# A two-layer hybrid decoder trunk: hand-over times per layer, rotary tables made first, row halves alternating in the Gram and score products

## The chip, the cores and the metric

The kernel runs on one core of one Trainium2 chip. The metric is the device time of one execution in microseconds (us); smaller is better. The core has a matrix engine (TensorE, PE in the profile; its weight loads are PEld), a vector engine (VectorE, DVE), an activation engine (ScalarE, ACT), a general engine (GpSimd, POOL) and a queue that issues most transfers (SyncE, SP). Each engine takes its instructions in the order in which they stand in its queue.

## What is computed

Two decoder layers over 512 tokens of width 1024, float32. Each layer runs three mixers side by side on one projection, adds their sum, and then a SwiGLU:

```python
for l in range(DEPTH):                       # DEPTH = 2
    hn = rms_norm(h, attn_norm[l])
    proj = hn @ w_in[l]                      # 1024 -> 2592
    y_a, v_first = rwkv7_mixer(...)          # 4 heads x 64, a delta-rule state per token
    y_b = retention_mixer(...)               # 4 heads x 64, chunks of 128, rotary q and k
    y_c = mla_mixer(...)                     # 8 heads, latent q / kv, one rotary key for all
    h = h + concat(y_a, y_b, y_c) @ w_out[l]
    gu = rms_norm(h, ffn_norm[l]) @ w_gate_up[l]
    h = h + (silu(gu[..., :D_FF]) * gu[..., D_FF:]) @ w_down[l]   # D_FF = 2816
return rms_norm(h, final_norm)
```

The RWKV-7 mixer's recurrence, for each head and token t, is

```python
sa = einsum('bhvk,bhk->bhv', state, -kkt)
state = state * wt + sa (x) (kkt * at) + vt (x) kt
y = einsum('bhvk,bhk->bhv', state, rt)
```

with kk the key direction brought to unit length. Rotary embedding multiplies by cos and sin of position times frequency.

## The kernel before

**Activations and GEMMs.** Activations lie transposed, channels on the 128 partitions and the 512 tokens along the row. Each weight block of 1024x128 (512 KB) is loaded by SP into a tile wr, rounded by ACT into wh (line 375) and its remainder formed into wl by DVE or POOL (line 376). An activation is kept as two such halves as well, and a product is three passes (high by high, high by low, low by high), 24 matmuls of 128x512 for a block: tiles pd<-u,wh and pd<-u,wl, all of them at line 231, the helper mm. Transposes are at line 238, the helper tr.

**What sets the order on PE.** `dense` is the main stream: it walks through the GEMMs of both layers. Beside it run tasks, Python generators: `tables` (cos and sin), `rwkv`, `chain`, `group_norm`, `retnet`, eight `head` tasks, `attend`, `key_rope`, `latent_norm`, `norm`. A `Driver` holds them with a priority and goes on with the first whose wait is over. A task yields either a condition or a number, the amount of modelled PE time that must pass before it continues; the numbers stand in the table T. So T sets where between the GEMM matmuls a task's products are put. PE keeps that order exactly; what the other engines do is ordered by a scheduler that follows from the same program.

**The RWKV task.** After the low-rank products (line 295 makes the halves of their input) it squares the scaled keys, sums them by head with a product by `blk` (the key norm: line 547 reads it, the rsqrt helper's lines 326 to 329 follow, line 548 multiplies), and forms decayed operands AR and BK per chunk of 64 tokens (DVE 605 to 607, POOL 608, 609). Then come the Gram matrices. Two heads share 128 partitions, 64 rows each (a row half, `par`); for each of 2 halves, 2 blocks and 2 chunk quartets, four matmuls of 64x128 go into one PSUM bank (tile pm), and DVE writes two masked copies of it (lines 632, 633, tiles GL and GR). Four PSUM banks serve all tiles named pm in turn. Behind the Gram matrices stand the bonus products (line 641 reads them) and the transposes of BK. A substitution of 31 steps of two DVE operations (lines 679, 680) inverts triangles; then the chain runs over eight chunks, with a copy R on ACT (729), a negated copy uv on ACT (733) and the state Sb on DVE (746, 748) between its products.

**RetNet and the rest.** The q and k blocks are multiplied by the norm's factor rB (DVE, line 978), four transfers on SP swap the rotary halves, POOL multiplies by cos and sin (981, 982) and DVE adds (983). `retnet` builds three chunk states: transpose, a decayed copy kt (DVE 794), product, masked copy Rs; then the score products of 64 rows, four matmuls to a bank, one bank for each head. Line 817 of its norm forms the low half that the next product reads. `key_rope` rotates the shared MLA key with six small DVE operations (1010 to 1015, tile kro) and transposes it. `tables` reads the positions and makes three sets of angles, the RetNet ones, a token-major set for the shared key and the MLA ones; the operations at 435 to 450 reduce each angle, ACT takes the sine.

Of the kernel before, what the change touches and what calls it, by code (L numbers as in the profile page):

```python
# [44 lines left out]
def shape_constants():  # L45
    """Constants that depend on shapes and hyper-parameters alone."""
# [39 lines left out]
# rows of the parameter matrix (one row = 128 consecutive values of a parameter)  # L86
# [15 lines left out]
class Driver:  # L102
    """Orders the PE stream: the first task whose wait (in PE time, or a condition) is over goes on."""
# [25 lines left out]
def lay_out(inp):  # L129
    """The inputs as the kernel reads them: reshapes, transposes and repeated columns only."""  # L130
# [47 lines left out]
def tile_trunk(ctx: ExitStack, tc: tile.TileContext, a: dict, out: bass.AP, dbg=None):  # L178
# [50 lines left out]
    def mm(o, lhsT, rhs, start=True, stop=True, cost=None):  # L229
        """A matmul that keeps its place in the PE stream."""  # L230
# [76 lines left out]
    def norm_feed(t, g, acc, tag="acc"):  # L307
        """Square of tile t into acc and the g-scaled tile as an exact hi/lo pair."""
# [14 lines left out]
    def rsqrt(x, y=None):  # L323
        """1 / sqrt(x) of a whole tile, with one Newton step."""
# [7 lines left out]
    def inv_rms(accs, n, tag):  # L332
        """rsqrt(mean + eps) per token, the same in all partitions, from tiles of squares."""
# [7 lines left out]
    def norm(acc, st):  # L341
        yield T["norm1"]
# [9 lines left out]
    # the weights, in order of use, as exact hi/lo pairs two blocks ahead of their products  # L352
# [31 lines left out]
    def gemm(ps, w, x, ks, first=True, last=True, wsl=None):  # L384
        """ps += w^T x in three exact passes; ks = [(index in w, index in x)]."""
# [13 lines left out]
    def first_two(x):  # L399
        """Two products whose last contraction tile comes late."""  # L400
# [16 lines left out]
    def tables():  # L417
        yield T["tables1"]
# [9 lines left out]
        def angles(inv, tok=False):  # L428
# [10 lines left out]
            yield T["angles1"]  # L439
            rest = TWO_PI  # L440
            for bits in (7, 9, 9, None):
# [7 lines left out]
                yield T["angles2"]  # L449
            dve.tensor_scalar(ang, ang, 3.1415925, -3.1415925, ALU.min, ALU.max)  # L450
            yield T["angles3"]
# [5 lines left out]
            yield T["angles4"]  # L457
# [7 lines left out]
        yield T["angles5"]  # L465
        yield from angles(None, True)
        ready["kr"] = True
        yield T["angles6"]
# [8 lines left out]
    def rwkv(l, st):  # L477
        rkv = st["rkv"]
        yield lambda: "xs1" in st
        yield T["rwkv1"]  # L480
# [16 lines left out]
        yield T["rwkv2"]  # L497
# [15 lines left out]
        yield T["rwkv3"]  # L513
        aa = ur([P, 2, S])
        gg = sm((P, 2, S), tag="gg", bufs=1)
        for rows, dst, bias in ((slice(32, 64), aa, "rw_a0"), (slice(64, 128), gg, None)):
            for b in range(2):
# [9 lines left out]
                yield T["rwkv4"]  # L527
        st["gg"] = gg

        # unit key direction  # L530
        yield lambda: "k" in rkv
        k_ = rkv["k"]
        yield T["rwkv5"]
# [8 lines left out]
        yield T["rwkv6"]  # L542
        for b in range(2):
# [5 lines left out]
            yield T["rwkv7"]  # L549
        # k' = k (1 + (a - 1) k_a),  b = kk a  # L550
# [10 lines left out]
        else:  # L561
            vf = ur([P, 2, S])
            sp.dma_start(vf, vf_d)
            yield T["rwkv8"]
# [5 lines left out]
            yield T["rwkv9"]  # L570
            for b in range(2):
# [7 lines left out]
                yield T["rwkv10"]  # L579

        # decays, centred on the middle of each chunk
# [6 lines left out]
        for b in range(2):  # L588
            Ein, Eex, Einv = r2(), r2(), r2()
            for i in range(2):  # L590
# [12 lines left out]
                yield T["rwkv11"]  # L603
# [12 lines left out]
        yield T["rwkv12"]  # L616
# [631 lines left out]
```

## Time and profile before

| | |
|---|---|
| median of 3 runs | 1428.18 us (1426.40 to 1428.36) |
| profiled execution, first to last instruction (its own time; no other is on the page) | 1423.1 us |
| instructions | 17218 |
| TensorE busy, matmuls | 1366.6 us, 96% |
| TensorE's weight loads | 1074.5 us, 76% |
| VectorE / ScalarE / GpSimd busy | 799.1 / 566.5 / 267.2 us |
| mean granted TensorE clock | 0.970 |
| moved by transfers | 130.85 MB, mean 92 GB/s |

The page states busy time per engine, and the granted clock as a share of full speed. A row of a timeline gives start, length, engine, line, operation, output<-inputs, shapes, count, and in brackets how long the engine was idle before it and whose result ended that. Matmuls are pipelined, so records overlap, and each float32 matmul of the small products shows as two records.

### The profile page before, as it was taken

The page shows a single profiled execution, that of the slowest core. Times are in us where ns is not written, and L with a number is a line of the kernel's source. Part 1 is how long each engine was busy: PE and PEld are TensorE (multiplying, and loading weights), DVE is VectorE, ACT ScalarE, POOL GpSimd, SP SyncE. Part 2 cuts the span into 40 slices and gives each one's busy share as a digit, 9 for nine tenths or more (in the row PEclk, how much of TensorE's full clock was granted, in tenths as well). Part 3 has the DMA queues.
Part 4 walks back from the last instruction along what each step waited for, and adds up shares of the span by engine and source line. Part 5 has one row for each costly group of instructions (what it writes and reads, how often), then busy time and mean ns, then how long its engine had stood idle before and what let it go on. Part 6 is the DMA issues. An engine that isn't in the chain of part 4 may idle for free.

```text
span 1423.1 us, 17218 instructions
## 1 busy us (share of the span) xinstructions
PE 1366.6 (96%) x6622; PEld 1074.5 (76%) x6622; DVE 799.1 (56%) x1167; ACT 566.5 (40%) x943; POOL 267.2 (19%) x233
## 2 busy tenths in 40 slices
PE   7989899899999999999999989999999999999996
PEld 5768666568788888888887776765788888888884
DVE  6665855775644345444556767657475434543443
ACT  7633353663432223222457134448263322322233
POOL 2142024222211011001213502332031200100111
PEclk9869999999999999999999899999999999999998
DMA  6324231202332232322342332312123333333321
GB/s 224 90 81 112 76 92 53 91 36 77 104 102 95 98 98 95 103 89 93 118 138 77 107 87 56 100 43 75 59 89 104 89 104 93 100 98 95 100 77 60
DMA packets 61738, 130.85 MB, mean 92 GB/s; under 512 B 24948, under 2 KB 27668, under 8 KB 61656
## 3 DMA queue, kind: packets, MB, share of 16 engines
q1 hardware_dynamic: 60280, 128.14, 29.1%
q8 instruction: 52, 0.85, 0.3%
q10 hardware_dynamic: 1232, 1.09, 0.2%
q0 software_dynamic: 144, 0.52, 0.1%
q14 instruction: 30, 0.25, 0.1%
HBM read 117.40 MB, written 9.18 MB: 89 GB/s over the span
## 4 chain that ended last, share of the span: by engine, by line
PE 83%; DVE 8%; ACT 4%; issue 3%; POOL 1%; DMA 0%; SPq 0%; DVEq 0%; ACTq 0%; POOLq 0%
PE pd L231 70%; PE pm L231 12%; PE pm L238 1%; DVE r L680 1%; ACT wh L375 1%; DVE u L320 1%; DVE r L679 1%; DMA wr<-in_wts_dram 0%; DVE wl L376 0%; ACT u L860 0%; DVE nmx L858 0%; DVE u L286 0%; DVE r L295 0%; DVE r L328 0%; DVE r L329 0%
## 5 line engine op out<-in xcount | busy, mean ns | idle before, releaser
L231 PE MATMUL pd<-u,wh 128*128 128x512 f32 x3048 | 963.6, 397 | 9.9 <-ACT wh L375 6.3
L231 PEld LDWEIGHTS pd<-u,wh 128*128 128x128 f32 x3048 | 571.2, 190 | 139.8 <-issue 8.3
L231 PE MATMUL pd<-u,wl 128*128 128x512 f32 x1524 | 598.8, 393 | 0.0
L375 ACT CAST wh<-wr 128x1024 fp32r<-128x1024 f32 (+3 forms) x206 | 208.6, 1015 | 547.0 <-PE pd L231 349.2
L231 PEld LDWEIGHTS pd<-u,wl 128*128 128x128 f32 x1524 | 289.3, 190 | 61.3 <-DVE wl L376 0.2
L376 DVE TENSOR_TENSOR wl<-wr,wh 128x1024 fp32r<-128x1024 f32 (+3 forms) x198 | 277.6, 1404 | 82.9 <-ACT wh L375 82.1
L1184 POOL TENSOR_TENSOR r<-r,r 128x512 f32<-128x512 f32 x44 | 62.3, 1416 | 584.3 <-ACT wh L375 337.5
L1183 DVE TENSOR_TENSOR r<-pd,rB 128x512 f32<-128x512 f32 x44 | 30.4, 691 | 133.7 <-PE pd L231 133.7
L1190 DVE TENSOR_TENSOR u<-u,pd 128x512 f32<-128x512 f32 x48 | 33.0, 687 | 125.8 <-PE pd L231 125.8
L231 PE MATMUL pm<-u,u 32*32 32x32 f32 (+7 forms) x856 | 97.3, 279 | 5.8 <-DVE u L607 4.3
L231 PEld LDWEIGHTS pm<-u,u 32*32 32x32 f32 (+4 forms) x856 | 70.1, 155 | 41.5 <-issue 25.2
L315 POOL TENSOR_TENSOR acc<-acc,r 128x512 f32<-128x512 f32 x37 | 56.8, 1534 | 221.5 <-ACT r L314 221.0
L1181 DVE TENSOR_TENSOR r<-pd,rB 128x512 f32<-128x512 f32 x44 | 30.4, 691 | 68.4 <-PE pd L231 68.3
L285 ACT CAST u<-r 128x512 fp32r<-128x512 f32 x52 | 32.2, 622 | 63.0 <-POOL r L1184 62.8
L231 PE MATMUL pd<-u,u 96*128 96x512 f32 (+3 forms) x128 | 47.7, 471 | 1.9 <-ACT u L860 1.3
L286 DVE TENSOR_TENSOR u<-r,u 128x512 fp32r<-128x512 f32 x52 | 36.4, 701 | 16.5 <-ACT u L285 16.3
L376 POOL TENSOR_TENSOR wl<-wr,wh 128x1024 fp32r<-128x1024 f32 (+1 forms) x8 | 19.7, 2460 | 116.8 <-ACT wh L375 98.9
L238 PE MATMUL pm<-ident,u 128*128 128x128 f32 x188 | 35.2, 295 | 2.7 <-ACT u L875 1.8
L858 DVE TENSOR_REDUCE nmx<-pd 128x1 f32<-128x512 f32 (+1 forms) x64 | 30.0, 481 | 12.1 <-PE pd L231 11.9
L320 DVE SCALAR_TENSOR_TENSOR u<-u,PC,u 128x512 fp32r<-128x512 f32 x24 | 34.5, 1450 | 3.0 <-ACT u L319 3.0
L238 PEld LDWEIGHTS pm<-ident,u 128*128 128x128 f32 x188 | 25.1, 153 | 9.5 <-ACT u L875 2.2
L745 POOL TENSOR_SCALAR sd<-Sb,dsc 64x64 f32<-64x64 f32 x48 | 23.9, 498 | 42.2 <-DVE Sb L746 33.6
(241 smaller groups left out, 1170.6 us busy)
## 6 DMA issues: line engine op xcount, KB each, us to landing
wr<-in_wts_dram SPq DMA_DIRECT2D x174, 512.0 KB, 3.5
wr<-in_wts_dram SPq DMA_DIRECT2D x22, 384.0 KB, 3.1
u<-in_xT_dram SPq DMA_DIRECT2D x7, 512.0 KB, 7.1
tb<-tab_d SPq DMA_DIRECT2D x8, 256.0 KB, 3.4
r<-r SPq DMA_DIRECT2D x32, 64.0 KB, 2.0
h_d<-u SPq DMA_DIRECT2D x4, 512.0 KB, 2.6
u<-h_d SPq DMA_DIRECT2D x4, 512.0 KB, 4.9
wr<-in_wts_dram SPq DMA_DIRECT2D x4, 432.0 KB, 3.1
```

Source lines behind the costliest of these rows:

```text
L231: tc.keep_in_program_order(nc.tensor.matmul(o, lhsT, rhs, start=start, stop=stop, skip_group_check=True))
L238: tc.keep_in_program_order(nc.tensor.transpose(o, x, idn))
L285: act.copy(hi, src)
L286: E("e273").tensor_tensor(lo, src, hi.bitcast(F32), ALU.subtract)
L315: E("e302").tensor_tensor(acc, acc, q, ALU.add)
L320: dve.scalar_tensor_tensor(lo, t, g, hi.bitcast(F32), ALU.mult, ALU.subtract)
L375: act.copy(hi[:, z], t[:, z])
L376: (pool if on in POOL_LO else dve).tensor_tensor(lo[:, z], t[:, z], hi[:, z].bitcast(F32), ALU.subtract)
L1181: dve.tensor_tensor(t, gu[0], rB, ALU.mult)
L1183: dve.tensor_tensor(u, gu[1], rB, ALU.mult)
L1184: E("e1171").tensor_tensor(t, t, u, ALU.mult)
L1190: dve.tensor_tensor(hk(m), hk(m), ps, ALU.add)
```

## The change

The table T becomes a list of two tables, one for each layer, and every task reads `T[l]`. Many of the numbers differ. Its start:

```diff
-T = {'tables1': 19.74, 'norm1': 0, 'p_rwkv': 4, 'p_ret': 1, 'p_head': 4, ...
+T = [{'tables1': 1.15, 'norm1': 0, 'p_rwkv': 4, 'p_ret': 0.66, 'p_head': 5.42, ...
+     {'norm1': 0, 'p_rwkv': 5.05, 'p_ret': 5.98, 'p_head': 0.39, ...
...
-        yield T["angles6"]
+        yield T[0]["angles6"]
```

Of the numbers in it, as before, layer 0 / layer 1: angles6 (before the MLA angles) 11 to 0; rwkv6 (before the key norm's products) 2 to 0 / 3.92; rwkv13 (between Gram steps) 0.5 to 1.32 / 0.1; retnet2 (between chunk states) 0 to 0 / 5.29; key_rope1 (before the key's transposes) 4.96 to 0 / 2.82. With tables1 and angles6 so small, the RetNet angles stand before the first norm's factor rB on DVE and the MLA angles before the Gram products, and the transfer of the positions stands ahead of two weight blocks on SP. In layer 0 the chain starts later in PE's order than before, behind the products that expand the queries.

The Gram products take both row halves in one step, alternating into two banks:

```diff
-        for par in range(2):
-            rows = slice(par * 64, par * 64 + 64)
-            for b in range(2):
-                for i in range(2):
-                    ps = psm()
-                    for j in range(4):
-                        n = 4 * i + j
-                        mm(ps[:, j * P : (j + 1) * P], BK[b][rows, n, :], AR[b][rows, n, :])
-                    h0 = b * 8 + 4 * i
-                    v3 = ps.rearrange("p (j w t) -> p j w t", j=4, w=2)
-                    dve.tensor_tensor(GL[par][...], v3[:, :, 0, :], ..., ALU.mult)
-                    dve.tensor_tensor(GR[par][...], v3[:, :, 1, :], ..., ALU.mult)
-                    yield T["rwkv13"]
-            sp.dma_start(ms_d[:, par * 16 : par * 16 + 16, :], GL[par][0:64])
+        GH = (slice(0, 64), slice(64, 128))
+        for b in range(2):
+            for i in range(2):
+                pg = [psm(), psm()]
+                for j in range(4):
+                    n = 4 * i + j
+                    for ps, rows in zip(pg, GH):
+                        mm(ps[:, j * P : (j + 1) * P], BK[b][rows, n, :], AR[b][rows, n, :])
+                h0 = b * 8 + 4 * i
+                v3 = [ps.rearrange("p (j w t) -> p j w t", j=4, w=2) for ps in pg]
+                for par in range(2):
+                    dve.tensor_tensor(GL[par][...], v3[par][:, :, 0, :], ..., ALU.mult)
+                    dve.tensor_tensor(GR[par][...], v3[par][:, :, 1, :], ..., ALU.mult)
+                yield T[l]["rwkv13"]
+        for par in range(2):
+            sp.dma_start(ms_d[:, par * 16 : par * 16 + 16, :], GL[par][0:64])
```

The score products of RetNet do the same, for each of the two blocks:

```diff
-            Sm = []
+            Sm, pg = [], [psm(), psm()]
+            for n in range(4):
+                tk = slice(n * P, (n + 1) * P)
+                for par in range(2):
+                    rows = slice(par * 64, par * 64 + 64)
+                    mm(pg[par][:, tk], ks[rows, b, tk], qs[rows, b, tk])
             for par in range(2):
-                hh = 2 * b + par
-                rows = slice(par * 64, par * 64 + 64)
-                ps = psm()
-                for n in range(4):
-                    tk = slice(n * P, (n + 1) * P)
-                    mm(ps[:, tk], ks[rows, b, tk], qs[rows, b, tk])
+                hh, ps = 2 * b + par, pg[par]
```

Comments are dropped and lines move by one to three (mm is line 232, the Gram copies 634 and 635, the RetNet rotary 981 to 986, the key rotary 1013 to 1018). What the change does to the order is seen at three places. The numbers at the end of a name tell buffers apart.

On PE, layer 0's Gram products: before, four matmuls of one half (pm<-u,u), then three GEMM matmuls of 512 columns (pd), eight times.

```order
L231 MATMUL pm_735<-u_632,u_633 128x128 x4
L231 MATMUL pd_702<-u_146,wh_505 128x512 x2
L231 MATMUL pd_702<-u_146,wl_506 128x512
L231 MATMUL pm_746<-u_632,u_633 128x128 x4
L231 MATMUL pd_764<-u_112,wh_600 128x512 x2
L231 MATMUL pd_764<-u_112,wl_601 128x512
L231 MATMUL pm_774<-u_673,u_674 128x128 x4
```

Now, from the last two matmuls of the first pair to the first two of the second:

```order
L232 MATMUL pm_756<-u_648,u_649 128x128
L232 MATMUL pm_757<-u_648,u_649 128x128
L232 MATMUL pd_718<-u_146,wh_565 128x512 x2
L232 MATMUL pd_718<-u_146,wl_566 128x512
L232 MATMUL pd_784<-u_112,wh_621 128x512 x2
L232 MATMUL pd_784<-u_112,wl_622 128x512
L232 MATMUL pd_784<-u_116,wh_621 128x512 x2
L232 MATMUL pd_784<-u_116,wl_622 128x512
L232 MATMUL pm_797<-u_648,u_649 128x128
L232 MATMUL pm_798<-u_648,u_649 128x128
```

Eight steps with 3 GEMM matmuls behind each became four pairs with 9; the number of GEMM matmuls ahead of the first stays at 96 from the low-rank products on.

On DVE, layer 0's key rotary (kro) and the substitution (r<-u,r and r<-r,r of growing size). Before:

```order
L450 TENSOR_SCALAR r_191_947<-r_191_947 128x512
L680 TENSOR_TENSOR r_189_924<-r_189_924,r_190_925 128x27x5
L1010 TENSOR_TENSOR kro_1133<-krt_967,ctk 128x4x16
L679 TENSOR_TENSOR r_190_925<-u_919,r_189_924 128x26x6
L1011 TENSOR_TENSOR kro_216_1134<-krt_967,stk 128x4x16
L680 TENSOR_TENSOR r_189_924<-r_189_924,r_190_925 128x26x6
```

Now:

```order
L377 TENSOR_TENSOR wl_1026<-wr_1024,wh_1025 128x1024
L377 TENSOR_TENSOR wl_1076<-wr_1074,wh_1075 128x1024
L1013 TENSOR_TENSOR kro_1129<-krt_948,ctk 128x4x16
L1014 TENSOR_TENSOR kro_217_1130<-krt_948,stk 128x4x16
L1015 TENSOR_TENSOR kro_1129<-krt_948,ctk 128x4x16
L1016 TENSOR_TENSOR kro_217_1130<-krt_948,stk 128x4x16
L1017 TENSOR_TENSOR kro_1129<-kro_1129,kro_217_1130 128x4x16
L1018 TENSOR_TENSOR kro_1129<-kro_1129,kro_217_1130 128x4x16
L682 TENSOR_TENSOR r_204_993<-u_987,r_203_992 128x31
```

The rotary's six operations moved from behind the MLA angles and between the substitution's steps to just ahead of its first. On PE the transposes of kro stood 27 GEMM matmuls behind the last V product, and now 3.

On DVE, layer 1's Gram evacuations (u<-pm,C) among RetNet's rotary (978, 983; now 981, 986). Before:

```order
L633 TENSOR_TENSOR u_6058<-pm_6090,C 128x256
L983 TENSOR_TENSOR u_5970<-u_5970,r_1180_6031 128x512
L632 TENSOR_TENSOR u_6057<-pm_6101,C 128x256
L633 TENSOR_TENSOR u_6059<-pm_6101,C 128x256
L978 TENSOR_TENSOR r_1195_6118<-pd_6040,rB_5522 128x512
```

Now:

```order
L981 TENSOR_TENSOR r_1193_6103<-pd_6040,rB_5522 128x512
L377 TENSOR_TENSOR wl_6121<-wr_6119,wh_6120 128x576
L634 TENSOR_TENSOR u_6068<-pm_6089,C 128x256
L635 TENSOR_TENSOR u_6070<-pm_6089,C 128x256
L634 TENSOR_TENSOR u_6069<-pm_6090,C 128x256
L986 TENSOR_TENSOR u_5942<-u_5942,r_1180_6031 128x512
L635 TENSOR_TENSOR u_6071<-pm_6090,C 128x256
L634 TENSOR_TENSOR u_6068<-pm_6128,C 128x256
```

Before, the first four of eight groups were copied out ahead of this line 983; now the first pair and all copies of the second but one, and that one (of pm_6090) stands behind it. On PE the pairs of layer 1 have 3 matmuls between them (512 columns behind the first, 288 behind the others), and start 12 GEMM matmuls later than the first group did. RetNet's products with kt there stand 33 and 27 GEMM matmuls apart, where 6 stood; between a transpose and the product with its kt stand 6, as before.

More of the change, by code (lines that the diff above doesn't have):

```diff
@@ L339, in inv_rms, with norm @@
         return rsqrt(x, sm((P, S), tag=tag, bufs=1))
-    def norm(acc, st):
-        yield T["norm1"]
+    def norm(l, acc, st):
+        yield T[l]["norm1"]
         st["rB"] = inv_rms(acc if isinstance(acc, list) else [acc], D, "rB")
@@ L417, in tables @@
     def tables():
-        yield T["tables1"]
+        yield T[0]["tables1"]
         posi = r2((P, S), I32)
@@ L456, in angles @@
             act.activation(si, ang, AF.Sin)
-            yield T["angles4"]
+            yield T[0]["angles4"]
             return co, si
@@ L479, in rwkv @@
         yield lambda: "xs1" in st
-        yield T["rwkv1"]
+        yield T[l]["rwkv1"]
         raw, w0b = r2((P, 256)), r2((P, 256))
@@ L496, in rwkv @@
         zh, zl = halves(z, "h1")
-        yield T["rwkv2"]
+        yield T[l]["rwkv2"]
         sig = ur([P, 4, 256])
@@ L532, in rwkv @@
         k_ = rkv["k"]
-        yield T["rwkv5"]
+        yield T[l]["rwkv5"]
         kk = ur([P, 2, S])
@@ L541, in rwkv @@
             sqs.append(halves(sq, "h2", sqf))
-        yield T["rwkv6"]
+        yield T[l]["rwkv6"]
         for b in range(2):
@@ L563, in rwkv @@
             sp.dma_start(vf, vf_d)
-            yield T["rwkv8"]
+            yield T[l]["rwkv8"]
             ps = psm()
@@ L569, in rwkv @@
             act.copy(t32, ps[0:32])
-            yield T["rwkv9"]
+            yield T[l]["rwkv9"]
             for b in range(2):
@@ L615, in rwkv @@
             ts[b] = halves(ts[b], "h3")
-        yield T["rwkv12"]
+        yield T[l]["rwkv12"]
         GL = [ur([P, 16, 64]) for _ in range(2)]
@@ L662, in rwkv @@
             UV.append(uv)
-            yield T["rwkv16"]
+            yield T[l]["rwkv16"]
         dg = ur([P, 32, 32])
@@ L699, in rwkv @@
             E("c686").copy(TQ[32:64, par * 16 : par * 16 + 16, :], ps[32:64].rearrange("p (j t) -> p j t", t=32))
-            yield T["rwkv19"]
+            yield T[l]["rwkv19"]
         for par in range(2):
-            yield T["rwkv20"]
+            yield T[l]["rwkv20"]
             ps = psm()
@@ L707, in rwkv @@
         st["chunk"] = (AR, BKT, UV, GL, GR, X, dsc)
-        yield T["rwkv21"]
+        yield T[l]["rwkv21"]
         for b in range(2):
@@ L729, in chain @@
             E("c716").copy(R, pR)
-            yield T["chain1"]
+            yield T[l]["chain1"]
             for par in range(2):
@@ L749, in chain @@
             E("c736").copy(AR[b][:, n, 64:128], pY)
-            yield T["chain3"]
-        drv.spawn(T["p_gn"], group_norm(l, st, b))
+            yield T[l]["chain3"]
+        drv.spawn(T[l]["p_gn"], group_norm(l, st, b))
     def group_norm(l, st, b):
@@ L756, in group_norm @@
         y = halves(y, "h4")
-        yield T["group_norm1"]
+        yield T[l]["group_norm1"]
         py = psm()
@@ L818, in retnet @@
                 Sm.append(t)
-                yield T["retnet3"]
-            yield T["retnet4"]
+                yield T[l]["retnet3"]
+            yield T[l]["retnet4"]
             py = psm()
@@ L841, in retnet @@
             split(q, mix[2 + b])
-            yield T["retnet6"]
+            yield T[l]["retnet6"]
     def head(l, st, b, par):
@@ L847, in head @@
         if hh < 3:
-            yield T["head1"]
+            yield T[l]["head1"]
         q_, k_ = st["qa"][b][:, par, :], st["ka"][b][:, par, :]
@@ L863, in head @@
             (pool if ib == 2 else dve).tensor_scalar(pp[ib], pp[ib], rs, None, ALU.mult)
-            yield T["head2"]
-        yield T["head3"]
+            yield T[l]["head2"]
+        yield T[l]["head3"]
         ta, tb = ur([P, 1024]), r2()
@@ L879, in head @@
         if hh ^ 1 in st["PT"]:
-            drv.spawn(T["p_att"], attend(l, st, b))
+            drv.spawn(T[l]["p_att"], attend(l, st, b))
     def attend(l, st, b):
-        yield T["attend1"]
+        yield T[l]["attend1"]
         po = psm()
@@ L931, in dense @@
             mix = st["mix"]
-            drv.spawn(T["p_rwkv"], rwkv(l, st))
-            drv.spawn(T["p_ret"], retnet(l, st))
+            drv.spawn(T[l]["p_rwkv"], rwkv(l, st))
+            drv.spawn(T[l]["p_ret"], retnet(l, st))
             for hh in range(8):
-                drv.spawn(T["p_head"], head(l, st, hh // 2, hh % 2))
+                drv.spawn(T[l]["p_head"], head(l, st, hh // 2, hh % 2))
             pss = yield from first_two(xg)
-            drv.spawn(0, norm(acc, st))
+            drv.spawn(0, norm(l, acc, st))
             ps = psd()
@@ L1022, in key_rope @@
                 st["kr"] = kr
-            drv.spawn(T["p_kr"], key_rope(krt))
+            drv.spawn(T[l]["p_kr"], key_rope(krt))
             rg = ur([P, 2, S])
@@ L1162, in dense @@
             del st["rB"]
-            drv.spawn(0, norm(acc, st))
+            drv.spawn(0, norm(l, acc, st))
             ps = psd()
```

55 lines of the change are left out of this document (28 added, 27 removed).

## The prediction

> **What bounds the kernel now.** I read the busy times first, then the chain that ended last, the windows with the granted clock, and the waits of TensorE (PE). Lines are those of the kernel before.
>
> ```profile
> PE 1366.6 (96%) x6622; PEld 1074.5 (76%) x6622; DVE 799.1 (56%) x1167; ACT 566.5 (40%) x943; POOL 267.2 (19%) x233
> PE 83%; DVE 8%; ACT 4%; issue 3%; POOL 1%; DMA 0%; SPq 0%; DVEq 0%; ACTq 0%; POOLq 0%
> ```
>
> PE is busy for 96% of the span and carries 83% of the chain, so a term counts only if it is PE work, a PE wait or PE's clock. The GEMMs stay as they are. The windows show where clock is lost (columns: stretch, length, busy us and count of PE, PEld, DVE, ACT, POOL, granted clock, DMA share, GB/s):
>
> ```profile
> 0.00:14.60 14.60, 8.07 (x16) 5.00 (x17) 7.01 (x12) 8.90 (x14) 1.80 (x12) 1.00 0.84 290
> 82.90:113.60 30.70, 30.70 (x94) 22.61 (x94) 15.51 (x30) 2.77 (x5) 5.89 (x6) 0.50 0.24 62
> 144.30:151.10 6.80, 4.08 (x12) 3.21 (x13) 6.70 (x21) 5.35 (x7) 0.46 (x1) 0.50 0.26 86
> 755.30:803.10 47.80, 46.30 (x211) 34.17 (x211) 39.04 (x46) 25.70 (x46) 26.95 (x17) 1.00 0.27 85
> 803.10:816.70 13.60, 13.60 (x52) 11.88 (x52) 6.98 (x14) 0.42 (x2) 5.41 (x7) 0.50 0.46 122
> ```
>
> Layer 0's Gram products run 30.7 us at half clock with PE never idle; at full clock that is 15.35 us of work, so 15.35 are lost. Layer 1's run from 791 at full clock and lose it at 803.1: 6.8 lost. The waits (engine, line, releaser, total, times, longest):
>
> ```profile
> PE pm L238 <- DVE kro L1015: 6.6, 1, 6.6
> PE pm L231 <- DVE kt L794: 5.5, 5, 3.0
> PE pm L231 <- DVE u L607: 4.3, 1, 4.3
> PE pm L231 <- DVE r L817: 2.8, 2, 1.7
> PE pm L231 <- DVE u L633: 1.5, 1, 1.5
> ```
>
> **When the clock falls.** TensorE's timeline, layer 0, layer 1, and plain GEMM matmuls:
>
> ```profile
> 82.10 1.34 PE L231 MATMUL pm<-u,u 64*128 64x128 f32 x8 [4.30 <-DVE u L607]
> 84.95 2.07 PE L231 MATMUL pm<-u,u 64*128 64x128 f32 x8
> 88.53 2.07 PE L231 MATMUL pm<-u,u 64*128 64x128 f32 x8
> 111.58 1.06 PE L238 MATMUL pm<-ident,u 128*128 128x128 f32 x4
> 791.45 1.16 PE L231 MATMUL pm<-u,u 64*128 64x128 f32 x8
> 793.43 1.16 PE L231 MATMUL pm<-u,u 64*128 64x128 f32 x8
> 800.93 1.13 PE L231 MATMUL pm<-u,u 64*128 64x128 f32 x8 [1.50 <-DVE u L633]
> 815.51 1.05 PE L238 MATMUL pm<-ident,u 128*128 128x128 f32 x4
> 272.61 0.63 PE L231 MATMUL pd<-u,wh 128*128 128x512 f32 x2
> 273.30 0.63 PE L231 MATMUL pd<-u,wh 128*128 128x512 f32 x2
> ```
>
> Both falls follow a wait (4.30 and 1.50 us) beside products that use 64 of 128 rows. Three GEMM matmuls take 0.69 us (272.61 to 273.30). A group of one half's four products with three GEMM matmuls behind it takes 1.98 us at full clock (791.45 to 793.43) and 3.58 at half (84.95 to 88.53); without the GEMM part 1.3 and 2.2, so 0.4 us of a group is fixed and 0.9 goes with the clock. Layer 1 kept full clock over four such periods, so the mixture alone does not take the clock; in layer 0 it did not bring it back.
>
> **Layer 0's Gram products.** Timelines of DVE and POOL:
>
> ```profile
> 67.09 2.47 DVE L328 SCALAR_TENSOR_TENSOR r<-r,r 128x512 f32<-128x512 f32 x1 [3.66 <-ACT r L327]
> 81.28 0.68 DVE L607 TENSOR_TENSOR u<-u,r 128x512 f32<-128x512 f32 x1
> 89.99 0.41 DVE L632 TENSOR_TENSOR u<-pm,C 128x256 f32<-128x256 f32 x1
> 90.32 0.41 DVE L633 TENSOR_TENSOR u<-pm,C 128x256 f32<-128x256 f32 x1
> 90.15 1.27 POOL L981 TENSOR_TENSOR u<-r,tb 128x512 f32<-128x512 f32 x1 [6.45 <-DVE r L978]
> 94.20 1.29 POOL L982 TENSOR_TENSOR r<-r,tb 128x512 f32<-128x512 f32 x1 [0.86 <-DMA r<-r]
> ```
>
> The key norm's products now stand 12 matmuls earlier, so less of the 3.66 us that DVE idled before L328 should remain. I let L607 end 2.5 us earlier, near 79.5, and PE wait 1.7 instead of 4.3: −2.6. From there DVE paces. Call the first pair's start G. The first evacuation comes 8.0 us after L607's end, as before (the same operations stand between), and one every 0.33, four to a pair: the third pair gets its banks at G+9.4. PE is ready for it at G+6.7 if the halves overlap wholly (two pairs of 1.3, 18 GEMM matmuls 4.1) and at G+8.5 if they go in turn (pairs of 0.4+1.8), so overlap buys nothing here: a new wait of 0.9 to 2.7 stands instead. The third pair is evacuated by G+12.9; then come L978 (0.6), POOL's two products (1.3 each), L983 (0.6), L978 (0.6), a weight half (1.0) and the last pair's first two evacuations: G+19 for the first transpose, against 29.5 before (82.10 to 111.58). 12 GEMM matmuls more, 2.7 us, lie within. −29.5+19−2.7 = −13.2, with the earlier G −15.8. A short window at half clock may give 1 back: I take −15. Ends: −18 (DVE two us earlier still), −4 (rival B).
>
> **Layer 0's key rotary.**
>
> ```profile
> 138.40 1.77 DVE L448 SCALAR_TENSOR_TENSOR r<-r,r 128x512 f32<-128x512 f32 x1
> 144.84 0.21 DVE L1010 TENSOR_TENSOR kro<-krt,ctk 128x64 f32<-128x64 f32 x1
> 146.75 0.21 DVE L1015 TENSOR_TENSOR kro<-kro,kro 128x64 f32<-128x64 f32 x1
> ```
>
> Six operations of 0.21 us stood behind angle arithmetic (1.77 each beside other work) and between the substitution's; now they stand ahead of the substitution, whose start waits for them. PE's cover falls from 27 GEMM matmuls (6.2 us) to 3 (0.7). The six take about 1.3 us without the others between (6×0.21), and the copy of krt on ACT comes first, bounded by 1 us: a wait of 1.6 remains, −5. Of the window 144.30 to 151.10, 4.08 us busy at half clock, 2 come back if 1.6 does not take the clock; I take 1.5. Together −6.5 (ends −7, −2). The substitution starts later, but has no angle operations between its steps; PE did not wait for its end before, so this is nothing.
>
> **Pairs of score products.** Two pairs per layer replace four groups. In turn a pair costs 2.2 for two groups' 2.6: −1.6 over four pairs. Wholly side by side 1.3: −5.2. No two row halves alternate in this trace; the nearest rows are column halves that do (second row), against products of the same length in one position:
>
> ```profile
> L231 PE MATMUL pm<-u,u 64*64 64x64 f32 x128 | 13.7, 229 | 0.0
> L231 PE MATMUL pm<-u,u 128*64 128x64 f32 x128 | 10.3, 244 | 0.0
> ```
>
> Per record 107 ns of busy time against 80, a ratio of 0.75: a pair 1.75, −3.4. I take −3. The Trainium skill ("TensorE: Matmul & The Clock Gate", Part 3) says that matmuls on different row tiles overlap and gives 3.07 times for four tiles; by that the four pairs give −5.2 and the sum is 2 us lower, which no run here shows.
>
> **Layer 1's Gram products.** DVE paces these already:
>
> ```profile
> 799.44 0.68 DVE L978 TENSOR_TENSOR r<-pd,rB 128x512 f32<-128x512 f32 x1
> 806.85 0.69 DVE L983 TENSOR_TENSOR u<-u,r 128x512 f32<-128x512 f32 x1 [4.08 <-POOL r L982]
> ```
>
> From L978 over a transfer and POOL to L983 pass 7.4 us. In the new order the second pair's last evacuation stands behind that L983, and only three matmuls lie between pairs. The first pair's banks come free at 801.4 (L978, then four evacuations), the second's at 807.5, the last is evacuated near 811. PE waits some 3 and 4 us and the clock probably falls. Transposes start near 811, not 815.5, with 9 matmuls of 288 columns (1.2 us) left to do: −3.3; a later return of the clock gives back about 1.3: −2 (ends −9, +3).
>
> **Layer 1's RetNet.**
>
> ```profile
> 845.65 0.71 PE L231 MATMUL pm<-u,kt 128*128 128x128 f32 x4 [2.99 <-DVE kt L794]
> 851.49 0.71 PE L231 MATMUL pm<-u,kt 128*128 128x128 f32 x4 [0.76 <-DVE kt L794]
> ```
>
> The state steps now stand 33 and 27 GEMM matmuls apart instead of 6, but between a transpose and the product with its kt there are still 6 (1.4 us). What ends these waits is DVE's queue: kt stands behind substitution steps and the state's own operations. Those of the step before now have time to finish, so the second and third wait should shrink (0.76 the longer); the first may keep most of its 2.99. The longer of L817's two waits (1.7) has more work around it. I take −2 of some 6 us in all (ends −6, +3).
>
> **What it adds.** Layer 0's chain starts after the query expansion: five or six of its eight steps lie among the heads' score products, where there were two. One such step, and its wait:
>
> ```profile
> 256.80 1.44 PE L231 MATMUL pm<-u,u 128*64 128x64 f32 x12
> 262.89 0.44 PE L231 MATMUL pm<-R,u 64*64 64x64 f32 x4 [0.41 <-ACT R L729]
> 264.28 0.45 PE L231 MATMUL pm<-u,u 128*64 128x64 f32 x8
> ```
>
> Four more steps with one or two such waits: +2 (ends 0, 7). On SP the positions (256 KB, 0.9 us at the 290 GB/s of the first window) go ahead of two weight blocks; nine DVE operations and a table load stand before the first norm's factor; the earlier key norm may wait for its halves: +2 (ends 0, 5).
>
> **Sum.** −15 −6.5 −3 −2 −2 +2 +2 = −24.5, from a profiled span of 1423.1. The runs' median of 1428.2 is 5.1 above that span; I carry the difference over: 1403.7, forecast 1404. About 0.2% (3 us) is what a measurement of this kernel can tell from no change.
>
> **Rivals.** A, the forecast: layer 0 holds its clock; chance 0.50, its own range 1397 to 1412.
>
> B: the clock falls in layer 0's Gram after all. For it: a new wait of up to 2.7 where 1.50 sufficed at 800.93; against it: more full-row work between. 36 GEMM matmuls at half clock are 16.6 us, four pairs 8.8 (overlapped) to 16, the bonus products 2: about 30 in place of 19, 1415. Chance 0.22. The Trainium skill ("TensorE: Matmul & The Clock Gate", Part 1) lets the clock return after some 3.4 us of sustained work. By that B would cost 2 us, not 11; the row 82.90:113.60, busy throughout at 0.50, does not agree, so B stands.
>
> C: the ends together: row halves overlap, DVE is early, layer 1 keeps its clock (a further −6.8) and RetNet's waits go: 1393. Chance 0.15. Against it stands the 7.4 us from L978 to L983.
>
> D, slower: the chain among layer 0's heads waits and takes the clock. Six steps of 7.5 us (256.80 to 264.28) are 45 us; 18 hand-overs at 0.41 add 7.4, and half clock over all of it up to 30, less the 24.5: 1441. It passes no change where half clock holds for some 26 of the 45 us (17 us of loss beside the 7.4). Against it: the two such steps before kept full clock. Chance 0.08. The remaining 0.05 lies between B and no change.
>
> From these, faster 0.88, same 0.04, slower 0.08. The range leaves out D and the far side of C: 1389 to 1419.
>
> **What would show it.** Right: clock 1.00 from 82 to 100 and transposes near 99; the key rotary's wait under 2 us; the pairs' products of both halves starting together, a pair in under 1.8; the later kt waits gone. Wrong: half clock through layer 0's Gram (B); a wait before the rotary's transposes as long as before; waits on R, uv or Sb among the heads of over 10 us (D).

## The result, and the profile after

The changed kernel takes 1391.71 us (median of 4 runs, 1390.35 to 1392.69); the kernel before took 1428.27 beside it. The ratio is 0.9752, 95% interval 0.9736 to 0.9768: faster by 36.6 us. The profiled span is 1390.9 us; the profiled run's own time, 1392.69, is 1.8 us above it. First the busy times, the waits of TensorE, and windows of the changed kernel (columns as before):

```profile
PE 1338.0 (96%) x6622; PEld 1054.3 (76%) x6622; DVE 799.1 (57%) x1167; ACT 563.9 (41%) x941; POOL 266.6 (19%) x233
```

```profile
PE pm L232 <- DVE u L635: 7.3, 5, 2.6
PE pd L232 <- ACT wh L376: 6.4, 1, 6.4
PE pm L232 <- DVE kt L797: 5.7, 5, 2.4
PE pm L239 <- ACT u L878: 3.2, 3, 1.8
PE pm L232 <- ACT r L293: 2.3, 2, 1.9
PE pm L232 <- DVE r L820: 1.9, 1, 1.9
```

```profile
79.00:97.00 18.00, 15.40 (x107) 11.80 (x108) 17.12 (x30) 6.25 (x9) 7.36 (x6) 1.00 0.35 105
152.50:159.30 6.80, 6.80 (x26) 4.55 (x26) 4.61 (x9) 2.77 (x5) 1.39 (x2) 0.50 0.21 58
777.20:787.40 10.20, 7.79 (x35) 6.51 (x35) 6.58 (x16) 0.59 (x1) 5.91 (x8) 0.50 0.65 171
```

PE is as full as before (96%) and busy for 28.6 us less: by the split below 13.9 are less work and 14.7 less time lost to half clock. Layer 0's Gram stage runs at full clock in this execution, in 18 us, and VectorE is busy for 17.1 of them. The waits for L607, the key rotary's 6.6 and L633's 1.5 are replaced by waits for the Gram copies (L635, 7.3 in five). TensorE's timeline of the places that the prediction named:

```profile
78.99 1.25 PE L232 MATMUL pm<-u,u 64*128 64x128 f32 x16 [0.64 <-DVE u L608]
82.46 1.16 PE L232 MATMUL pm<-u,u 64*128 64x128 f32 x16
87.77 0.46 PE L232 MATMUL pm<-u,u 64*128 64x128 f32 x2 [1.89 <-DVE u L635]
96.68 0.63 PE L239 MATMUL pm<-ident,u 128*128 128x128 f32 x4 [0.50 <-PE pm L232]
117.47 0.60 PE L239 MATMUL pm<-ident,kro 128*32 128x128 f32 x4 [1.07 <-DVE r L682]
152.12 0.43 PE L232 MATMUL pm<-r,u 128*64 128x128 f32 x2 [1.87 <-DVE r L820]
775.25 0.46 PE L232 MATMUL pm<-u,u 64*128 64x128 f32 x2 [2.57 <-DVE u L635]
781.05 2.04 PE L232 MATMUL pm<-u,u 64*128 64x128 f32 x14 [2.41 <-DVE u L635]
785.61 1.05 PE L239 MATMUL pm<-ident,u 128*128 128x128 f32 x4
816.24 0.71 PE L232 MATMUL pm<-u,kt 128*128 128x128 f32 x4 [2.43 <-DVE kt L797]
826.56 0.71 PE L232 MATMUL pm<-u,kt 128*128 128x128 f32 x4 [1.85 <-DVE kt L797]
```

Sixteen records of both halves take 1.16 us, what eight of one half took before (791.45): the halves run side by side.

To see where the time went I split each profiled span in three: idle is the span less PE's busy time; lost is half of PE's busy time within all stretches at granted clock 0.50; work is the rest, PE's busy time brought to full clock.

| kernel | median us | span | idle | lost | work |
|---|---|---|---|---|---|
| before | 1428.3 | 1423.1 | 56.5 | 35.0 | 1331.6 |
| changed | 1391.7 | 1390.9 | 52.9 | 20.3 | 1317.7 |
| pairs in turn | 1392.3 | 1389.8 | 47.1 | 20.2 | 1322.6 |
| alternation only, old times | 1434.2 | 1436.9 | 77.9 | 42.5 | 1316.5 |
| old times, pairs in turn | 1436.2 | 1430.9 | 70.5 | 35.0 | 1325.4 |
| new times only | 1414.2 | 1416.0 | 56.1 | 27.7 | 1332.2 |
| tables only | 1421.5 | 1419.3 | 54.3 | 35.6 | 1329.4 |
| changed, layer 1 on old times | 1407.8 | 1407.4 | 60.7 | 28.8 | 1317.8 |
| changed, tables back | 1399.5 | 1396.8 | 58.9 | 22.4 | 1315.5 |
| changed, key norm late | 1398.3 | 1391.4 | 53.9 | 20.7 | 1316.8 |

Of the 32.2 us between the two profiled spans, 14.7 are clock, 13.9 work (overlapped products) and 3.6 waits. The other 4.4 between the medians are not in the profiles: the profiled execution of before (1423.1 and 1.8 make 1424.9) lies below that median, the one of the changed kernel above its own. The new stretch at 152.5 and its wait were not foreseen. The parts of each row belong to its one profiled execution, which need not be the median one: with the alternation only it was the slowest of five (1438.7), with the new times only the second slowest of six (1417.8), with the key norm late the fastest of four (1393.2).

### The profile page after: what moved, and what is told of

It reads as the page before. It is cut to its first block, busy times and chain, and to the rows that moved or that the text cites. A ratio compares the mean times of both kernels' runs of the same rounds, so it can differ in the third digit from the quotient of the medians.

```text
span 1390.9 us, 17204 instructions
## 1 busy us (share of the span) xinstructions
PE 1338.0 (96%) x6622; PEld 1054.3 (76%) x6622; DVE 799.1 (57%) x1167; ACT 563.9 (41%) x941; POOL 266.6 (19%) x233
## 4 chain that ended last, share of the span: by engine, by line
PE 80%; DVE 6%; ACT 2%; issue 2%; POOL 1%; DMA 0%; SPq 0%; DVEq 0%; POOLq 0%; ACTq 0%
PE pd L232 69%; PE pm L232 10%; PE pm L239 1%; DVE r L682 1%; DVE u L321 1%; DVE r L683 1%; DVE nmx L861 0%; ACT u L863 0%; DVE wl L377 0%; POOL r L1187 0%; DVE r L1222 0%; DVE u L1160 0%; ACT u L878 0%; DVE r L296 0%; ACT wh L376 0%
## 5 line engine op out<-in xcount | busy, mean ns | idle before, releaser
L232 PEld LDWEIGHTS pd<-u,wl 128*128 128x128 f32 x1524 | 288.1, 189 | 60.7 <-DVE wl L377 0.2
L232 PE MATMUL pm<-u,u 32*32 32x32 f32 (+7 forms) x856 | 81.0, 276 | 10.0 <-DVE u L635 7.3
L232 PEld LDWEIGHTS pm<-u,u 32*32 32x32 f32 (+4 forms) x856 | 54.4, 149 | 42.3 <-issue 27.4
L287 DVE TENSOR_TENSOR u<-r,u 128x512 fp32r<-128x512 f32 x52 | 36.5, 702 | 15.4 <-ACT u L286 15.3
L377 POOL TENSOR_TENSOR wl<-wr,wh 128x1024 fp32r<-128x1024 f32 (+1 forms) x8 | 20.2, 2526 | 87.0 <-ACT wh L376 65.6
L866 POOL TENSOR_SCALAR u<-u,rs 128x384 f32<-128x384 f32 x16 | 20.4, 1272 | 50.9 <-DVE rs L865 49.2
```

What stands on the lines that cost most here:

```text
L232: tc.keep_in_program_order(nc.tensor.matmul(o, lhsT, rhs, start=start, stop=stop, skip_group_check=True))
L377: (pool if on in POOL_LO else dve).tensor_tensor(lo[:, z], t[:, z], hi[:, z].bitcast(F32), ALU.subtract)
```

## The experiments

In all of them the reference for "before" was run in the same job: its medians there were 1426.5 (first four), 1427.3 (next four) and 1426.8 (last four).

**One half after the other.** The order of the two inner loops is exchanged, in the Gram and in the score products:

```diff
-                for j in range(4):
-                    n = 4 * i + j
-                    for ps, rows in zip(pg, GH):
+                for ps, rows in zip(pg, GH):
+                    for j in range(4):
+                        n = 4 * i + j
```

> The changed kernel with the two halves of a pair one after the other (four products of rows 0 to 63, then four of rows 64 to 127) in the Gram and the score products; everything else, the places in TensorE's order too, is the same. Theory 1 (overlap is worth only its own time, the clock is kept by the short waits): a pair costs 0.9 us more; hidden in layer 0's and most of layer 1's Gram stage, where VectorE paces, and paid in the four score pairs: +3.6 to +6 us over the changed kernel, about 1396, clock 1.00 from 82 to 100. Rival (streaming all 128 rows is what keeps the clock): the clock falls in layer 0's Gram stage at the third pair's wait and stays down: +10 us or more, 1402 to 1408.

1392.3 us (ratio 0.9761, 0.9749 to 0.9774), against 0.9752 for the changed kernel: no difference that can be measured, better than theory 1 by 4 us and against the rival. Its window and its first and third pair:

```profile
79.00:97.00 18.00, 17.08 (x110) 13.91 (x110) 17.14 (x31) 6.18 (x9) 6.44 (x6) 1.00 0.34 101
```

```profile
78.78 1.68 PE L232 MATMUL pm<-u,u 64*128 64x128 f32 x16 [0.80 <-DVE u L608]
87.56 1.79 PE L232 MATMUL pm<-u,u 64*128 64x128 f32 x16 [0.92 <-DVE u L635]
96.31 0.60 PE L239 MATMUL pm<-ident,u 128*128 128x128 f32 x4
```

A pair takes 1.7 us instead of 1.2, and not the 2.3 of two separate groups (1.16 each at 791.45), so even in turn the second half starts while the first runs: in the second pair the second half's first record starts at 83.21, the first half's last one at 83.54. The wait at the third pair is shorter by as much (0.92 for 1.89 and 0.21), the transposes start no later (96.31 to 96.68), and VectorE is busy for 17.1 of 18 us in both. In the table PE has 4.9 us more work and 5.8 us less idle time. Full clock in layer 0's Gram stage doesn't need the alternation.

**The alternation without the new times.** T is the old table for both layers, the rest is the changed kernel:

```diff
-T = [{'tables1': 1.15, ...}, {...}]
+T = [{'tables1': 19.74, ...}] * 2      # the table of the kernel before
```

> The alternation of the changed kernel with the hand-over times and the table order of the kernel before, in both layers. Theory 1: the 4.3 us wait ahead of layer 0's Gram products stays and the clock falls there as before, but full rows let it return within one or two windows of 3.4 us; with overlapped pairs and the score pairs 12 to 18 us of the 36.5 appear, 1410 to 1416; the 6.6 us wait for the key rotary stays. Rival (the times alone made the gain): half clock through the Gram stage as before, 3 to 6 us for overlap alone, 1422 to 1425.

1434.2 us, ratio 1.0056 (1.0043 to 1.0069): slower than before, which neither theory had. In the profiled execution work falls by 15 us, as in the changed kernel, but idle time rises by 21 and the clock loses 7.5 more. Its waits:

```profile
PE pm L238 <- DVE kro L1017: 9.6, 1, 9.6
PE pm L231 <- DVE u L634: 9.6, 2, 5.6
PE pm L231 <- DVE r L819: 6.1, 2, 3.4
PE pm L231 <- DVE u L607: 4.3, 1, 4.3
```

Products that take half the time reach VectorE's results earlier: Gram pairs wait for copies (4.0 us at layer 0's third pair, 5.6 in layer 1), the key rotary's transposes 9.6 instead of 6.6. The saved work turned into waits, and these took the clock with them.

**The times without the pairs.** The new T with the old loops (and half of rwkv13, as there are twice as many steps):

```diff
-T = {'tables1': 19.74, ...}
+T = [{'tables1': 1.15, ...}, {...}]    # the tables of the changed kernel
-                    yield T["rwkv13"]
+                    yield T[l]["rwkv13"] / 2
```

> The hand-over times and table order of the changed kernel with the Gram and score loops of the kernel before (one half at a time; the time between Gram steps halved, since there are twice as many). Theory 1: the wait ahead of layer 0's Gram is under 1 us, so the clock holds there as it did in the first part of layer 1's Gram stage before; 8 groups of 1.3 us instead of 4 pairs of 1.3: +2 to +6 in the Gram stages, +5 for the scores: 1398 to 1404. Rival (full rows keep the clock): half clock returns to layer 0's Gram stage, 1410 to 1418.

1414.2 us (0.992, 0.9905 to 0.9935). Its windows:

```profile
78.00:108.00 30.00, 29.45 (x172) 24.10 (x173) 22.85 (x37) 10.91 (x16) 14.53 (x13) 1.00 0.46 126
119.90:126.70 6.80, 4.08 (x12) 3.23 (x13) 3.62 (x11) 0.57 (x1) 2.08 (x3) 0.50 0.26 77
867.40:884.50 17.10, 16.42 (x121) 12.96 (x118) 9.54 (x15) 6.07 (x11) 5.85 (x4) 0.50 0.05 10
976.60:983.40 6.80, 6.03 (x19) 2.31 (x19) 2.67 (x4) 2.52 (x4) 1.26 (x1) 0.50 0.00 0
```

The place bears theory 1 out (the rival wanted half clock in layer 0's Gram stage, and half-row groups ran there at full clock all through, after a wait of 0.57), but the size bears the rival's 1410 to 1418 out: the time comes from elsewhere, a rotary wait of 4.9 us with its window, and windows near 867 and 976. The order that the Driver makes from these numbers depends on the modelled length of the products between them; with the old loops the same numbers put tasks at other places.

**The tables alone**, in the kernel before:

```diff
-T = {'tables1': 19.74, ..., 'angles4': 0.65, 'angles5': 2.78, 'angles6': 11.0, ...
+T = {'tables1': 1.15, ..., 'angles4': 0, 'angles5': 2.18, 'angles6': 0, ...
```

> The kernel before with the rotary tables made first (tables1 1.15, angles4 0, angles5 2.18, angles6 0) and nothing else. Theory 1: layer 0's wait for the key rotary (6.6 us) and its half-clock window go, -7 to -9 us; layer 0's Gram stage stays at half clock: 1419 to 1422. Rival: the angle operations ahead of the Gram stage delay its operands, the wait there grows by 2 to 5 us and nothing is won, 1426 to 1432.

1421.5 us (0.9942, 0.9918 to 0.9965): faster by 5 of 1426.5, a little under theory 1. Its twelve executions spread over 16 us, those of no other kernel over more than 8: four took 1408.3 to 1413.3 us at a mean granted clock of 0.977 to 0.982, eight took 1417.1 to 1424.6 at 0.968 to 0.974. The profiled one (1421.1) is of the second kind; where the others kept the clock is not known. In it the rotary's wait falls from 6.58 to 2.47; a wait for kt of 2.17 comes in its place. Layer 0's Gram stage stays at half clock for 27.3 us, behind a wait of 2.60.

**The old times with the pairs in turn**, both edits above together.

> The pairs of the changed kernel under the hand-over times of the kernel before, as in the run with the alternation alone, but with the two halves of a pair one after the other. In the run with the alternation alone the clock fell after the 4.30 us wait at 81.18 and was back within two windows of 3.4 and 6.8 us, where the kernel before stayed at half clock for 30.7 us. Theory 1 (alternating row halves, which stream all 128 rows, bring the clock back): in turn it stays down for 15 us or more from 82, and the time is 4 to 8 us above the 1434 of that run. Rival (a pair in turn overlaps enough, or the denser GEMM matmuls between pairs do it): half clock for under 12 us there, time within 3 us of 1434.

The time, 1436.2 (1.0067, 1.005 to 1.0084), can't be told from 1434.2. The clock can. Windows of the run with the alternation and old times, then of this one:

```profile
82.20:85.60 3.40, 3.40 (x21) 2.43 (x20) 3.40 (x5) 1.53 (x2) 0.58 (x1) 0.50 0.00 0
85.60:89.00 3.40, 1.23 (x9) 0.63 (x7) 2.59 (x5) 0.62 (x1) 0.00 (x0) 1.00 0.61 152
89.00:95.80 6.80, 4.95 (x25) 3.84 (x27) 5.29 (x14) 0.00 (x0) 3.70 (x3) 0.50 0.31 93
95.80:106.00 10.20, 10.20 (x68) 8.60 (x65) 4.25 (x10) 5.48 (x9) 2.16 (x5) 1.00 0.68 124
```

```profile
82.60:103.10 20.50, 19.31 (x80) 15.35 (x79) 15.35 (x30) 2.05 (x3) 6.73 (x9) 0.50 0.36 92
```

Both fall after the same wait (4.30 and 4.31 us). With alternating halves the clock is back after 3.4 us, and again 6.8 us after the next wait; in turn it stays down for 20.5, with PE busy for 19.3 of them. So in these two executions the half of theory 1 about the clock stands: with the halves alternating the clock came back, with one half at a time it did not. That the rows in use decide is not shown. In the changed kernel's stretch at 152.50 every product uses all 128 rows, part of them with 64 of 128 columns (128*64), PE is busy for 6.80 of 6.80 us, and the clock is back only after 6.8:

```profile
L232 PE MATMUL pm<-r,Rs 128*128 128x128 f32 x6 | 2.4, 499 | 0.0
L232 PE MATMUL pm<-r,u 128*64 128x128 f32 x13 | 2.4, 435 | 0.0
L232 PE MATMUL pd<-u,wh 128*128 128x512 f32 x4 | 2.3, 670 | 0.0
```

And alternating pays through the clock only where the clock has fallen.

**Layer 1 on the old table**, layer 0 as changed:

```diff
-     {'norm1': 0, 'p_rwkv': 5.05, 'p_ret': 5.98, 'p_head': 0.39, ...}]
+     {'tables1': 19.74, 'norm1': 0, 'p_rwkv': 4, 'p_ret': 1, 'p_head': 4, ...}]    # the table of the kernel before
```

> The changed kernel with layer 1 on the one table of the kernel before (layer 0 keeps its new numbers, the pairs stay in both layers). Theory 1 (the new times matter because the pairs need other gaps; layer 1 alone lost 6 us of span in the profile with its new times, and gained 10 in the run with the alternation alone and old times): +10 to +18 us, 1402 to 1410, with waits of 4 us or more at the Gram pairs and at the chain's end in layer 1. Rival (layer 1's numbers hardly matter, the pairs do): within 4 us of the changed kernel.

1407.8 us (0.9854, 0.9828 to 0.9879), 16 above the changed kernel, as theory 1 has it. The waits in layer 1 grow, that at its Gram pairs to

```profile
PE pm L232 <- DVE u L635: 7.6, 3, 5.5
PE pm L232 <- DVE r L820: 5.3, 2, 3.4
PE pm L239 <- ACT u L878: 5.2, 4, 2.4
```

and the table shows 7.8 more idle and 8.5 more lost. So with the pairs in place layer 1's new numbers are worth these 16 us. Whether one new table for both layers would do as well was not run.

**The tables back** at their old places, in the changed kernel's layer 0:

```diff
-T = [{'tables1': 1.15, ..., 'angles4': 0, 'angles5': 2.18, 'angles6': 0, ..., 'key_rope1': 0, ...
+T = [{'tables1': 19.74, ..., 'angles4': 0.65, 'angles5': 2.78, 'angles6': 11.0, ..., 'key_rope1': 4.96, ...
```

> The changed kernel with the rotary tables at their old places (tables1 19.74, angles4 0.65, angles5 2.78, angles6 11, key_rope1 4.96 in layer 0); the rest as changed. Theory 1 (the early tables take the key rotary's wait away and leave VectorE free for the substitution): the wait before the rotary's transposes is 5 us or more again, with a half-clock window: +6 to +10 us, 1398 to 1402. Rival (the wait went because the substitution starts later, whatever the tables do): +0 to +3 us.

1399.5 us (0.9806, 0.9791 to 0.9821), 7.8 above the changed kernel: theory 1's size, at another place. The rotary does not wait; kt does, and so does the first Gram pair:

```profile
PE pm L232 <- DVE kt L797: 9.9, 4, 4.9
PE pm L232 <- DVE u L608: 2.8, 1, 2.8
```

The edit also moves the rotary's transposes back behind more GEMM matmuls (key_rope1), so the 7.8 us belong to both changes. I read it so: the early tables free VectorE at this time, and who waits without them depends on the order.

**The key norm of layer 0 late again**, in the changed kernel:

```diff
-'rwkv6': 0      # layer 0
+'rwkv6': 2.0
```

> The changed kernel with the key norm's products of layer 0 where they stood before (rwkv6 2.0 instead of 0), 12 GEMM matmuls later. Theory 1 (the clock in layer 0's Gram stage hangs on the length of the wait ahead of it): the wait at the first pair grows from 0.6 to 3 us or more and the clock falls there, but full rows let it return within two windows: +3 to +7 us, 1395 to 1399. Rival (the wait does not grow, VectorE being late for another reason): within 2 us of 1392.

1398.3 us (0.9789, 0.977 to 0.9808; single runs from 1393.2 to 1398.9), +6.6. The first pair waits 2.60 us instead of 0.64, and two windows of 3.4 us fall to half clock:

```profile
80.80:84.20 3.40, 3.40 (x9) 2.72 (x9) 3.40 (x6) 1.53 (x2) 0.42 (x1) 0.50 0.00 0
84.20:91.00 6.80, 5.35 (x43) 3.91 (x42) 5.99 (x13) 3.66 (x5) 1.26 (x1) 1.00 0.48 140
91.00:94.40 3.40, 3.40 (x9) 2.70 (x9) 2.54 (x7) 0.12 (x1) 1.69 (x2) 0.50 0.57 190
```

The wait, the windows and the time are theory 1's. But the profiled execution took 1393.2, against 1392.7 for the changed kernel's, with the wait and both windows in it. The other three took 1398.3 to 1398.9 at a mean granted clock of 0.974 instead of 0.980. So the 6.6 us of the median go with the clock, and no profile here shows at which place.

**Four single numbers of the changed kernel**, each in a run of its own, in this order:

```diff
-'retnet2': 5.29     # layer 1
+'retnet2': 0
-'rwkv13': 0.1       # layer 1
+'rwkv13': 0.7
-'retnet4': 0        # layer 0
+'retnet4': 2.0
-'retnet1': 0.8      # layer 1
+'retnet1': 2.2
```

> The changed kernel with layer 1's RetNet chunk states close together again (retnet2 0 instead of 5.29 in layer 1). Theory 1 (spreading gained little, since the waits for kt of 2.43 and 1.85 us remain in the changed kernel: VectorE's queue sets them): within 3 us of the changed kernel, 1390 to 1396. Rival (the spread is what layer 1 gained): +5 us or more, with three waits for kt of 3 us and under, and one of 2 to 3 us at the scores.

1391.3 us (0.975, 0.9736 to 0.9764): theory 1. The spread of RetNet's states gained nothing.

> The changed kernel with more modelled time between layer 1's Gram pairs (0.7 instead of 0.1: one to two more 288-column triples between them). Theory 1 (VectorE and the rotary behind it pace the pairs there): the two waits of 2.57 and 2.41 us shrink by what is put between, the end of the stage does not move: within 3 us of the changed kernel unless the clock stays up (-3 to -5). Rival (the waits are lost time): -2 to -4 us.

1397.7 (0.9795, 0.9781 to 0.9808): 6 slower, neither theory. The two Gram waits fall to 1.8 and 1.5 as meant, but what follows in layer 1 moves; one wait appears and one grows (at L840, from 0.3):

```profile
PE pm L232 <- ACT r L765: 3.7, 1, 3.7
PE pm L232 <- ACT r L840: 3.0, 1, 3.0
```

> The changed kernel with retnet4 2.0 instead of 0 in layer 0, which puts 18 GEMM matmuls instead of 12 between the second pair of score products and the product that reads their masked copies. Theory 1 (the wait of 1.87 us there took the clock for 6.8 us): wait under 0.7, window gone, -3 to -5 us, 1387 to 1389. Rival (the clock falls anyway, on the 64-row score products): the window stays, -1 us or nothing.

1395.8 (0.9785, 0.9771 to 0.9798): 4 slower, neither. The wait of 1.87 goes, but a latent's norm product now comes where it waits for POOL's sum of squares:

```profile
PE pm L232 <- POOL acc L316: 3.7, 2, 3.0
```

> The changed kernel with retnet1 2.2 instead of 0.8 in layer 1, which puts more GEMM matmuls between a transpose of the keys and the product with their decayed copy kt. Theory 1 (those products wait for VectorE's queue behind the substitution): the waits of 2.43 and 1.85 us fall to 1 or less, -2 to -4 us. Rival (later state steps delay the scores and their norm, which then wait in their place): within 2 us or slower.

1391.3 (0.9752, 0.974 to 0.9765): the rival. The waits for kt shrink (5.3 in six, the longest 1.5), and one of 3.7 for L765, a group norm's squares, appears near the layer's end. No version beat the changed kernel by more than the spread of its executions.

## Why the prediction was right, and where it was off

The time lies in the range and the direction was right, but the forecast of 1404 was 12 us high, and 1391.7 is below the range given to A itself (1397 to 1412), at rival C's 1393. C's number came without all of C: the halves overlap wholly and VectorE was early, but layer 1 did not keep its clock and RetNet's waits did not go. By steps, in the profiles:

- **Layer 0's Gram products**: −15 forecast. From PE's arrival to the first transpose, 77.80 to 111.58 before (33.8) and 78.35 to 96.68 (18.3), with 12 more GEMM matmuls (2.8) inside: −18.2. The schedule held: first wait 0.64 (1.7 forecast), the third pair waiting 1.89 (0.9 to 2.7), transposes 17.7 us after G (19). VectorE paced, and the overlap bought nothing, as the run with the halves in turn shows. The clock did not fall in the profiled execution, so rival B did not come.
- **The key rotary**: −6.5. The wait went from 6.58 to 1.07 (−5.5) and its half-clock window went (−2): −7.5. The six operations take 0.9 us (116.42 to 117.32 on VectorE) and not the 1.3 of 6×0.21, since they start 0.14 apart; the wait is for them, though the view names L682, which stands right behind them.
- **What was missed**: the masked scores of RetNet. With retnet4 0 instead of 3.0 in layer 0 there are 12 GEMM matmuls between them and their use; the wait for L820 grew from 1.1 to 1.87 and took the clock for 6.8 us, all of it busy (152.50): +4.2. The 3.4 of clock in it differ from one execution to the next. Up to 735 us the runs that alter layer 1 alone have the same products on PE in the same order as the changed kernel, and the wait here is 1.86 to 1.89 us in all five; behind it the clock stood at half for 6.8 us (changed kernel, retnet2 0), for 3.4 (rwkv13 0.7, layer 1 on the old table) or not at all (retnet1 2.2). In one of the five it fell for 3.4 us in layer 0's Gram stage too, behind the third pair's wait. The run with retnet1 2.2 here, then that with layer 1 on the old table in the Gram stage:

```profile
151.60:158.40 6.80, 6.63 (x34) 4.07 (x34) 6.23 (x12) 4.19 (x8) 2.14 (x2) 1.00 0.19 58
90.30:93.70 3.40, 3.40 (x10) 2.19 (x10) 2.62 (x5) 0.44 (x1) 2.31 (x2) 0.50 0.51 180
```

- **Score pairs**: −3, taken from the column halves' 0.75. The halves overlap wholly: a pair with nine GEMM matmuls has a period of 3.47 (78.99 to 82.46), so a pair costs 1.4 instead of 2.6, −4.8 over four. The Trainium skill's rule on row tiles ("TensorE: Matmul & The Clock Gate", Part 3), −5.2 by the prediction's working, was the better one here.
- **Layer 1's Gram products**: −2. The transposes start 29.9 us earlier, 26.0 of which layer 0 had gained (the same GEMM matmul opens the stretch ahead at 719.0 and 693.1), with 1.2 of work left over: −2.7. The two waits were 2.57 and 2.41 for 3 and 4, and the clock fell, as forecast.
- **Layer 1's RetNet**: −2. The waits for kt stayed (4.2 before, 4.3 now), layer 1's at L817 went (−1.7). That the later two waits would shrink was wrong: one grew from 0.48 to 1.85, the other (0.76) went. The run with retnet2 0 shows the step itself to be worth nothing.
- **What it adds**: +4. The chain waits for R 0.2 us in all, and the key norm 0.7: the two costs were oversized by some 3 us. Rival D did not come.
- **From the span to the runs**: I carried over 5.1 us from the profiled span of before to its median. For the changed kernel the median is 0.8 above the span, which makes another 4.3.

The profiled terms make −30.0 of the span's −32.2; 2.2 us are not assigned. The reading of the two clock falls (a wait beside half-row work) agrees with the runs with the key norm late and with old times, where the clock fell behind waits of 2.60, 4.30 and 4.31 us. It is not the whole: behind one and the same wait the clock fell in some executions and not in others, and it fell without any wait behind the low-rank products (last section). The rule of the Trainium skill that was set against it ("TensorE: Matmul & The Clock Gate", Part 1: back after some 3.4 us of sustained work) holds in the run with alternating halves (3.4 us at 82.20) and fails with halves in turn (20.5 at 82.60, PE busy for 19.3).

The larger surprise is none of the terms: times and pairs were added up as if each had its own worth. Alone the pairs cost 7.7 us (1426.5 to 1434.2), the times alone, which with the old loops make another order, give 12.4, and together 36.6.

## What to carry to other kernels

When products get shorter in a stream whose order is set by modelled time, set the times again with them; here the times alone gave a third of the gain and the shorter products alone a loss. Ask of every saved microsecond of the busiest engine who delivers its next operand: where VectorE's copies set the pace, twice as fast products only wait, and a wait beside half-row products can cost more through the clock than by itself: in the kernel before, 4.30 us of wait stood ahead of 15.4 us lost to the clock, and 1.50 ahead of 6.8. Since the same wait takes the clock in one execution and not in the next, compare several executions before giving a few us to one place. A single number that removes one wait can put another task in front of its operand, so judge it by the whole run.

## What the runs showed of the hardware

Products on rows 0 to 63 and 64 to 127 into two banks run side by side. The group of these 192 records, in the kernel before, the changed one and the one with the halves in turn:

```profile
L231 PE MATMUL pm<-u,u 64*128 64x128 f32 x192 | 36.9, 349 | 5.8 <-DVE u L607 4.3 <-DVE u L633 1.5
```

```profile
L232 PE MATMUL pm<-u,u 64*128 64x128 f32 x192 | 17.0, 304 | 7.9 <-DVE u L635 7.3 <-DVE u L608 0.6
```

```profile
L232 PE MATMUL pm<-u,u 64*128 64x128 f32 x192 | 23.4, 309 | 3.4 <-DVE u L635 2.6 <-DVE u L608 0.8
```

36.9 us of busy time became 17.0 and 23.4; part of each figure, of the first above all, is half clock. That order in turn overlaps too was not expected. The stretches at half clock are multiples of about 3.4 us (3.4, 6.8, 10.2, 20.5, 30.7). They began behind waits from 1.25 us (third pair, key norm late) to 4.31 beside the Gram or score products, though not behind every such wait (1.89 at 87.77 in the changed kernel). In layer 0's Gram stage of before (half-row groups, three full-row matmuls between) it stayed at half for 30.7 us with PE busy throughout. A stretch can also begin with no wait at all: in layer 1 of the changed kernel, behind low-rank products over 32 of 128 rows, with PE busy all the time:

```profile
723.55 2.82 PE L232 MATMUL pm<-r,LR 32*128 32x512 f32 x10
719.00:726.00 7.00, 7.00 (x38) 5.30 (x36) 4.38 (x6) 3.57 (x6) 0.00 (x0) 1.00 0.33 109
726.00:729.40 3.40, 3.40 (x9) 2.48 (x8) 1.83 (x2) 3.40 (x6) 0.00 (x0) 0.50 0.00 0
```

The kernel before has the same at 751.90.
